# Forgetting scores negated, their mask and minimum in one VectorE instruction, the softmax division moved to the branch, and the output halves added in DRAM

## The chip, the cores and the metric

The kernel runs on one core of a Trainium2 chip. The metric is the device time of one execution in microseconds (us), smaller being better. Three executions of the kernel before took 1705.4, 1707.59 and 1708.07 us; the median is 1707.59 us.

## What is computed

One decoder block in float32 on 1024 tokens of width 1024: three gated attention branches, merged, projected and added to the residual, and then a squared-ReLU MLP. The lines that matter here:

```python
# stick-breaking: 8 heads of 64, strictly causal
log_rem = jnp.where(strict, jax.nn.log_sigmoid(-z), 0.0)
w = jnp.where(strict, jnp.exp(jax.nn.log_sigmoid(z) + after), 0.0)
# forgetting: 8 heads of 64, F = cumsum(log_sigmoid(f_logit + b_forget))
z = z + F[:, :, q0:kend, None] - F[:, :, None, :kend]
p = jax.nn.softmax(jnp.where(causal, z, NEG_INF), axis=-1)
# memory: 4 heads of 128 on 256 memory tokens, ordinary softmax
merged = gates[:, :, 0] * br_sb + gates[:, :, 1] * br_fox + gates[:, :, 2] * br_mem
x = x + jnp.einsum('bsd,de->bse', merged, w_out[l])
u = jax.nn.relu(jnp.einsum('bsd,df->bsf', h2, w_ff_up[l]))
x = x + jnp.einsum('bsf,fd->bsd', u * u, w_ff_down[l])
```

## The kernel before

Each matmul operand is split into a high and a low float32r part, and a product is the sum of three matmuls (high by high, high by low, low by high). The work has five stages: a prologue that norms and turns the tokens; the input projections; attention together with the gate projections; the three branch products and the output projection; the MLP's two products.

Up to the end of the branches the order of the instructions is not written out: the kernel runs a small planner (`Machine`) while it is built. Each piece of work is a generator that asks for a place (`Get`, a tile or a PSUM bank) or for an engine (`Op`, with an engine, an assumed cost and a function that emits the instructions). The planner emits them in the order in which its own model would start them, and the chip then runs each engine's list strictly in that order. Pieces marked `side=True`, the dense gate and branch products of L1119, are taken on TensorE only when no attention piece is ready, so they fill the gaps of attention.

The attention stage has 64 units: 4 head pairs of stick-breaking (`sb_tile`), then 4 of forgetting (`fox_tile`), each with 2 heads by 4 groups of two query blocks of 128. A unit makes two tiles of scores (128 queries by 128 to 1024 keys), in chunks of at most 512 columns, one PSUM bank each, and then, in `unit`, turns them on TensorE (L904, through the bank `tr`), splits them into `pth` (ScalarE, L909) and `ptl` (VectorE, L911), and multiplies by V (L921). V lies as high and low halves side by side, so the product has the high half's result in partitions 0 to 63 and the low half's in 64 to 127, and the two must be added.

A forgetting chunk before: two matmuls (L837, L838; the second adds F by four extra rows `fq_scr`, `fk_scr`), on the last chunk an addition of the triangle mask `above` to its last 128 columns (L843), the row maximum (L844), its negation (L845), and the exponential with the row sum accumulated (L848). A tile of two chunks then brings the chunks to one maximum with small VectorE instructions and one small exponential (L856, L858), makes 1/sum (L862 to L865), and ScalarE multiplies the tile by it (L871). A tile of one chunk has a reciprocal (L867) in place of those.

At a unit's end ScalarE copies the low half to `ob` (L939), VectorE adds the high half (L940), and SP stores the 64 by 256 result to `o_scr` (L942). `ob` has three tiles. GpSimd (POOL) issues the loads of this stage: queries and keys (L979), values (L1015), memory operands (L567, L577) and the weights of the dense work, `raw<-w_in` (L1037), which ScalarE and VectorE then split (L1029, L1030).

After attention, `bring` loads each 128 rows of a branch's `o_scr` into `raw` (L1554) and splits them; `dense_branch` runs the memory and stick-breaking branches, and `last_branch` the forgetting branch.

Of the kernel before, what the change touches and what calls it, by code (L numbers as in the profile page):

```python
# [43 lines left out]
def tile_hybrid_block(  # L44
# [40 lines left out]
    C = Pool("c", st=32, st16=8, ss=4)  # L85
# [10 lines left out]
    def mmbank():  # L96
# [6 lines left out]
    above = C.p.tile([P, P + 1], F32, tag="above", name="above")  # L103
    nc.gpsimd.memset(above, 0.0)
    nc.gpsimd.affine_select(out=above, in_=above, pattern=[[-1, P + 1]], compare_op=ALU.is_ge,
                            fill=NEG, base=0, channel_multiplier=1)
    tri, strict = above[:, :P], above[:, 1:]
# [10 lines left out]
    o_scr = [dram.tile([512, S], F32, name=f"o_scr{b}", tag=f"o_scr{b}") for b in range(3)]  # L118
    gate_scr = dram.tile([3 * D, S], F32, name="gate_scr", tag="gate_scr")
# [11 lines left out]
    def stat(n, dt=F32):  # L131
        return (C.t("st", [P, 8], dt) if n <= 8 else C.t("st16", [P, 16], dt))[:, :n]

# [203 lines left out]
    ES, OO, EL, RR, HT, PH, PL, OB, VV, BK = (Places([]) for _ in range(10))  # L337
# [127 lines left out]
    def small_loads():  # L465
# [9 lines left out]
        def scale():  # L475
            nc.vector.tensor_scalar(gq2, gq2, HD ** -0.5, None, ALU.mult)
            nc.vector.tensor_scalar(gmq, gmq, P ** -0.5, None, ALU.mult)
# [116 lines left out]

    def mem_attention(h, half, kv, q):
# [8 lines left out]
        def scores_of(t2):  # L604
# [9 lines left out]
            def maxima():  # L614
                nc.vector.tensor_reduce(mx, sc.rearrange("p (t m) -> p t m", m=MEM), AX.X, ALU.max)
                nc.vector.tensor_scalar(mx, mx, -1.0, None, ALU.mult)
# [7 lines left out]
            yield Op("DVE", dve_time(512) + SMALL, maxima)  # L624
# [161 lines left out]
    def sb_tile(pair, b, i, beta):  # L786
# [4 lines left out]
        def chunk(ci, c, m, u):  # L791
# [6 lines left out]
            def sigmoids():  # L798
                nc.scalar.activation(rho[:, c:c + u], sc[:, :u], AF.Sigmoid, scale=-HD ** -0.5)  # L799
                nc.scalar.activation(beta[:, c:c + u], sc[:, :u], AF.Sigmoid, scale=HD ** -0.5)  # L800

            yield Op("PE", mm_time(m, m), scores)
            if c + u == n:
                dg = sc[:, u - P:u]
                yield Op("DVE", 0.22, lambda: nc.vector.tensor_tensor(dg, dg, strict, ALU.add))
# [18 lines left out]
    def fox_tile(pair, b, i, e):  # L824
# [5 lines left out]
        st = stat(16)  # L830
        mx, nx, l, f, t_, m = (st[:, c0:c0 + 2] for c0 in range(0, 12, 2))

        def chunk(ci, c, cols, u):
# [6 lines left out]
            def maxima():  # L840
                if c + u == n:
                    dg = sc[:, u - P:u]
                    nc.vector.tensor_tensor(dg, dg, tri, ALU.add)  # L843
                nc.vector.tensor_reduce(mx[:, ci:ci + 1], sc[:, :u], AX.X, ALU.max)  # L844
                nc.vector.tensor_scalar(nx[:, ci:ci + 1], mx[:, ci:ci + 1], -1.0, None, ALU.mult)  # L845
            yield Op("PE", mm_time(cols, cols), scores)
            yield Op("DVE", (0.22 if c + u == n else 0.0) + dve_time(u) + SMALL, maxima)
            yield Op("ACT", act_time(u) + 0.21, lambda: nc.scalar.activation(  # L848
                e[:, c:c + u], sc[:, :u], AF.Exp, bias=nx[:, ci:ci + 1], accum_out=l[:, ci:ci + 1]), table=AF.Exp)
# [4 lines left out]
        if two:  # L854
            def most():
                nc.vector.tensor_tensor(m[:, 0:1], nx[:, 0:1], nx[:, 1:2], ALU.min)  # L856
            yield Op("DVE", SMALL, most)
            yield Op("ACT", 0.22, lambda: nc.scalar.activation(f, mx, AF.Exp, bias=m[:, 0:1]), table=AF.Exp)  # L858

        def scale():  # L860
            if two:
                nc.vector.tensor_tensor(t_, l, f, ALU.mult)  # L862
                nc.vector.tensor_tensor(m[:, 1:2], t_[:, 0:1], t_[:, 1:2], ALU.add)
                nc.vector.reciprocal(t_[:, 0:1], m[:, 1:2])
                nc.vector.tensor_scalar(f, f, t_[:, 0:1], None, ALU.mult)  # L865
            else:
# [1712 lines left out]
```

## Time and profile before

| | us |
|---|---|
| median of three runs (1705.4 to 1708.07) | 1707.59 |
| the profiled execution | 1706.93 |
| its span, first to last instruction | 1705.1 |
| around the span | 1.83 |
| attention with the gate projections, from about | 380 to 850 |

The profile shows one execution. Its groups of instructions give busy time, the mean of one instruction in ns, and the idle time of the engine just ahead of them with what ended it. Busy time by stretches of the span shows where an engine had room, the view of waits shows who waited for whom, and the chain of waits follows the work that ended last back in time. TensorE's matmuls overlap: each is shown for some 390 ns, and the next one starts after some 230 ns at 512 columns. Matmul ends are modelled, so gaps shorter than this overlap do not show as idle time.

### The profile page before, as it was taken

Reading aid. Unit: us, or ns where it says so; the run is one execution under the profiler, and the core shown is the slowest. Engines: PE = TensorE matmul, PEld = TensorE weight load, DVE = VectorE, ACT = ScalarE, POOL = GpSimd, SP = SyncE. Lnnn points to the kernel's source line nnn. Section 1 sums busy time; section 2 is a strip of 40 time slices with the busy share of each in tenths; the row PEclk is TensorE's granted clock in tenths of the full one; section 3 lists DMA queues with packets and bytes.
Section 4 is the critical chain, followed back from the end, with each engine's and each line's share of the span. In section 5 each row is a group of like instructions: output and inputs, shape, how many; then the busy total and the mean of one; then the engine's idle time right before and its main releaser. Section 6 shows DMA issues by size and latency. Waiting matters only on the chain.

```text
span 1705.1 us, 25350 instructions
## 1 busy us (share of the span) xinstructions
PE 1691.7 (99%) x9186; PEld 1442.8 (85%) x9186; DVE 1346.3 (79%) x2321; ACT 886.8 (52%) x1635; POOL 256.0 (15%) x441
## 2 busy tenths in 40 slices
PE   9999999999999999999999999999999999999998
PEld 9998899998888888888888887878888887888887
DVE  7977678868999888888656898987777776788775
ACT  6445555556676798889733446533233344332331
POOL 0000000043322233241000011021211120000000
PEclk9999999999999999999999999999999999999999
DMA  7545444576544453553375642144444484554532
GB/s 242 162 144 191 135 124 149 157 245 187 160 128 123 113 176 112 183 164 110 100 238 168 217 179 94 56 162 141 156 153 149 142 289 180 195 206 148 198 123 74
DMA packets 131406, 271.72 MB, mean 159 GB/s; under 512 B 15761, under 2 KB 43409, under 8 KB 131281
## 3 DMA queue, kind: packets, MB, share of 16 engines
q1 hardware_dynamic: 99600, 169.94, 29.2%
q0 software_dynamic: 31680, 100.17, 19.5%
q8 instruction: 72, 1.18, 0.3%
q14 instruction: 54, 0.43, 0.1%
HBM read 181.44 MB, written 88.60 MB: 158 GB/s over the span
## 4 chain that ended last, share of the span: by engine, by line
PE 83%; issue 7%; DVE 5%; DMA 2%; POOL 2%; ACT 1%; SPq 0%; POOLq 0%; DVEq 0%; ACTq 0%
PE pp L1119 21%; PE pp L2518 7%; PE pp L1405 7%; PE pp L1848 6%; PE sc L1405 5%; PE tr L904 4%; PE tr L2518 4%; PE sc L2518 4%; PE sc L1119 3%; PE sc L1848 3%; PE pv L2518 2%; PE pv L921 2%; PE pp L921 2%; PE pv L1405 2%; POOL s_scr L1865 2%
## 5 line engine op out<-in xcount | busy, mean ns | idle before, releaser
L1119 PE MATMUL pp<-hi,whi 128*128 128x512 f32 x368 | 147.6, 401 | 0.0
L1119 PE MATMUL pp<-hi,wlo 128*128 128x512 f32 x368 | 145.0, 394 | 0.0
L1119 PE MATMUL pp<-lo,whi 128*128 128x512 f32 x368 | 144.8, 393 | 0.0
L1030 DVE TENSOR_TENSOR wlo<-raw,whi 128x1024 fp32r<-128x1024 f32 (+1 forms) x82 | 100.0, 1221 | 38.9 <-ACT whi L1029 38.6
L2518 PE MATMUL pp<-h,sop 128*128 128x512 f32 x540 | 128.7, 395 | 1.4 <-DVE sop L1784 1.4
L2518 PEld LDWEIGHTS pp<-h,sop 128*128 128x128 f32 x540 | 101.1, 187 | 26.5 <-DVE sop L1784 1.8
L1848 PE MATMUL pp<-h,oh 128*128 128x512 f32 x384 | 120.9, 396 | 0.7 <-ACT cu L1934 0.6
L1029 ACT ACTIVATE whi<-raw 128x1024 fp32r<-128x1024 f32 (+1 forms) x82 | 86.8, 1059 | 52.4 <-PE pp L1405 18.7
L911 DVE TENSOR_TENSOR ptl<-tr,pth 128x512 fp32r<-128x512 f32 (+1 forms) x160 | 98.8, 627 | 11.0 <-ACT pth L909 10.6
L909 ACT ACTIVATE pth<-tr 128x512 fp32r<-128x512 f32 (+1 forms) x160 | 86.7, 558 | 28.5 <-PE tr L904 15.5
L814 DVE TENSOR_TENSOR_SCAN r<-r,sm 128x896 f32<-128x896 f32 (+4 forms) x64 | 85.5, 1345 | 3.5 <-ACT r L799 3.4
L2436 ACT ACTIVATE h<-t 128x2048 fp32r<-128x2048 f32 x16 | 30.7, 1919 | 110.4 <-DVE t L1784 97.9
L1848 PEld LDWEIGHTS pp<-h,oh 128*128 128x128 f32 x384 | 71.7, 187 | 19.2 <-ACT cu L1934 1.5
L1119 PEld LDWEIGHTS pp<-hi,wlo 128*128 128x128 f32 x368 | 69.1, 188 | 16.4
L1119 PEld LDWEIGHTS pp<-lo,whi 128*128 128x128 f32 x368 | 69.5, 189 | 10.3
L1119 PEld LDWEIGHTS pp<-hi,whi 128*128 128x128 f32 x368 | 69.4, 189 | 10.1
L1848 PE MATMUL pp<-h,ol 128*128 128x512 f32 x192 | 75.9, 396 | 0.0
L1841 ACT ACTIVATE oh<-raw 128x512 fp32r<-128x512 f32 x64 | 39.4, 625 | 61.7 <-DVE raw L1784 61.7
L2518 PE MATMUL sc<-h,sop 128*128 128x512 f32 x264 | 63.4, 395 | 0.0
L2518 PE MATMUL tr<-h,sop 128*128 128x512 f32 x264 | 63.4, 395 | 0.0
L1784 DVE TENSOR_TENSOR sop<-ur,sop 128x2048 fp32r<-128x2048 f32 x27 | 61.7, 2286 | 1.7 <-ACT sop L2447 1.7
L844 DVE TENSOR_REDUCE st<-sc 128x1 f32<-128x512 f32 (+2 forms) x96 | 53.3, 555 | 9.3 <-PE sc L838 7.1
(586 smaller groups left out, 5102.9 us busy)
## 6 DMA issues: line engine op xcount, KB each, us to landing
ur<-s_scr SPq DMA_DIRECT2D x26, 1024.0 KB
raw<-w_in POOLq DMA_DIRECT2D x42, 512.0 KB, 5.2
raw<-w_up SPq DMA_DIRECT2D x60, 256.0 KB
s_scr<-s POOLq DMA_DIRECT2D x60, 256.0 KB, 2.5
g<-w_down SPq DMA_DIRECT2D x14, 1024.0 KB
s_scr<-cu POOLq DMA_DIRECT2D x48, 256.0 KB, 2.9
gate_scr<-o SPq DMA_DIRECT2D x44, 256.0 KB
o<-gate_scr SPq DMA_DIRECT2D x32, 256.0 KB
```

The costliest lines, as they stand in the source:

```text
L814: nc.vector.tensor_tensor_scan(out=rev, data0=rev, data1=zero.to_broadcast([P, n]), initial=1.0, op0=ALU.mult, op1=ALU.add)
L904: nc.tensor.transpose(tr[:, jj * 256 + a * P:jj * 256 + (a + 1) * P], es[a][:, j * P:(j + 1) * P], ident)
L909: yield Op("ACT", act_time(512 - lo_c), lambda: nc.scalar.activation(ph[:, lo_c:], tr[:, lo_c:], AF.Copy))
L911: yield Op("DVE", dve_time(512 - lo_c), lambda: nc.vector.tensor_tensor(pl[:, lo_c:], tr[:, lo_c:], f32(ph[:, lo_c:]), ALU.subtract))
L921: nc.tensor.matmul(pv[0][:, c_:256], pair.v[:, j, b, :], p_[:, jj * 256 + c_:(jj + 1) * 256], start=(k == 0 and n_ == 0 and i == 0), stop= ...
L1029: yield Op("ACT", 0.03 + act_time(m), lambda: nc.scalar.activation(hi, raw, AF.Copy))
L1030: yield Op("DVE", dve_time(m), lambda: nc.vector.tensor_tensor(lo, raw, f32(hi), ALU.subtract))
L1119: nc.tensor.matmul(ps, a_, b_, start=(first and i == 0), stop=(last and i == n - 1))
L1405: nc.tensor.matmul(out_, a_, b_, start=(first and n == 0 and j == 0), stop=(last and n == 3 and j == len(todo) - 1), skip_group_check=True)
L1784: nc.vector.tensor_tensor(out_, a_, b_, op)
L1848: nc.tensor.matmul(ps, w[a_][:, k * P:(k + 1) * P], h[b_][k], start=(first and k == 0 and i == 0), stop=(last and k == 3 and i == 2), skip ...
L2518: nc.tensor.matmul(ps, a_[:, c, qs], b_[:, c, :], start=(kind in ("P1", "P2", "P7") and c == 0 and i == 0), stop=(kind in ("P2", "P4", "P3 ...
```

## The change

- **Scores of the forgetting heads are made negative.** The query gain gets a factor of -1, and F's rows change their signs. A row's maximum becomes a minimum, which is the bias that the exponential needs (with scale -1), so that the negation goes.
- **Mask and minimum in one instruction.** On a tile's last chunk one `tensor_tensor_reduce` adds the mask and takes the minimum. The mask is a new tile `later` of 513 columns: zeros, with the triangle in the last 129, so that a slice of it ends in the triangle for each chunk width. The stick-breaking queries are negated as well, and their mask is the same triangle. In the order below this instruction is two rows, both named ISA.
- **One minimum for both chunks.** The second chunk's exponential takes the minimum of both as its bias; the first chunk alone is brought to it afterwards, on VectorE (512 columns), which also adds the two sums.
- **1/sum leaves the tile.** The sums stay in the columns of `fn`; at the end of a pair one reciprocal of 128 by 16 is taken and stored to `l_scr` in runs of 4 bytes (`sums_kept`). `bring` loads them spread over 64 partitions each (two DMAs) and VectorE multiplies the 128 by 1024 rows before they are split.
- **Output halves added by a DMA.** ScalarE copies all 128 partitions to `ob`. SP stores the high half, and POOL then issues a DMA that adds the low half to the same place in DRAM.
- The memory heads' negation goes into the reduction's `negate`.

```diff
             def maxima():
                 if c + u == n:
-                    dg = sc[:, u - P:u]
-                    nc.vector.tensor_tensor(dg, dg, tri, ALU.add)
-                nc.vector.tensor_reduce(mx[:, ci:ci + 1], sc[:, :u], AX.X, ALU.max)
-                nc.vector.tensor_scalar(nx[:, ci:ci + 1], mx[:, ci:ci + 1], -1.0, None, ALU.mult)
+                    nc.vector.tensor_tensor_reduce(sc[:, :u], sc[:, :u], holder["later"][:, 512 - u:512], 1.0, -NEG,
+                                                   ALU.add, ALU.min, nx[:, ci:ci + 1])
+                else:
+                    nc.vector.tensor_reduce(nx[:, ci:ci + 1], sc[:, :u], AX.X, ALU.min)
...
+            if ci == 0:
+                machine.fire(first_max)
+            else:
+                yield first_max
+                bias = m
+                yield Op("DVE", SMALL, lambda: nc.vector.tensor_tensor(m, nx[:, 0:1], nx[:, 1:2], ALU.min))
             yield Op("ACT", act_time(u) + 0.21, lambda: nc.scalar.activation(
-                e[:, c:c + u], sc[:, :u], AF.Exp, bias=nx[:, ci:ci + 1], accum_out=l[:, ci:ci + 1]), table=AF.Exp)
+                e[:, c:c + u], sc[:, :u], AF.Exp, scale=-1.0, bias=bias,
+                accum_out=l[:, ci:ci + 1] if two else total), table=AF.Exp)
...
-        def scaled():
-            for ci, (c, _, u) in enumerate(ch):
-                nc.scalar.activation(e[:, c:c + u], e[:, c:c + u], AF.Copy, scale=f[:, ci:ci + 1])
-        yield Op("DVE", SMALL * (4 if two else 1), scale)
-        yield Op("ACT", act_time(*[u for _, _, u in ch]) + 0.0002 * n, scaled)
+            yield Op("ACT", 0.22, lambda: nc.scalar.activation(f, nx[:, 0:1], AF.Exp, scale=-1.0, bias=m), table=AF.Exp)
+
+            def scaled():
+                nc.vector.tensor_scalar(e[:, :512], e[:, :512], f, None, ALU.mult)
+                nc.vector.scalar_tensor_tensor(total, l[:, 0:1], f, l[:, 1:2], ALU.mult, ALU.add)
+            yield Op("DVE", dve_time(512) + SMALL, scaled)
...
-        o = ob[:HD, :]
-        yield Op("ACT", act_time(256), lambda: nc.scalar.activation(o, pv[0][HD:P, :256], AF.Copy))
-        yield Op("DVE", dve_time(256), lambda: nc.vector.tensor_tensor(o, o, pv[0][0:HD, :256], ALU.add))
+        yield Op("ACT", act_time(256), lambda: nc.scalar.activation(ob, pv[0][:, :256], AF.Copy))
         PV.put(pv[0])
-        yield Op("SP", 0.1, lambda: nc.sync.dma_start(scr[r0:r0 + HD, g * 256:(g + 1) * 256], o), 2.5)
+        dst = scr[r0:r0 + HD, g * 256:(g + 1) * 256]
+        yield Op("SP", 0.1, lambda: nc.sync.dma_start(dst, ob[:HD, :]), 3.0)
+        yield Op("POOL", 0.6, lambda: nc.gpsimd.dma_start(dst, ob[HD:, :], accum_op=ALU.add), 3.5)
         OB.put(ob)
...
+    def sums_kept(h0):
+
+        cols = fn[:, 8 * h0:8 * h0 + 16]
+        yield Op("DVE", SMALL, lambda: nc.vector.reciprocal(cols, cols))
+        yield Op("SP", 0.4, lambda: nc.sync.dma_start(
+            l_scr[h0:h0 + 2, :].rearrange("h (i p) -> p (h i)", p=P), cols, allow_slow_non_contiguous=True), 4.0)
...
+        def issue():
+            nc.sync.dma_start(raw[:, :S], src)
+            if bi == 2:
+                for i, half in enumerate((slice(0, HD), slice(HD, P))):
+                    nc.sync.dma_start(sums[half, :], l_scr[2 * k + i:2 * k + i + 1, :].partition_broadcast(HD))
+        yield from transfer(issue, P * S * (8 if bi == 2 else 4))
+        if bi == 2:
+            yield Op("DVE", dve_time(S), lambda: nc.vector.tensor_tensor(raw[:, :S], raw[:, :S], sums, ALU.mult))
+            RR.put(sums)
```

With other costs and other pieces the planner emits another order. TensorE has the same 8855 rows, ScalarE 1368 in place of 1454, VectorE 2028 in place of 2290, POOL 452 in place of 390, SP 508 in place of 500. Three places; line numbers of the order after are those of the changed file (L843, L844: the score matmuls; L905: the turns; L922: the products by V; L1122: dense and memory products; L861: the exponential).

**TensorE, the turns of the narrow tile of the last forgetting unit.** The tile is `es_4095` before, `es_4093` after, 256 keys wide. Before, the rows ahead of its turns:

```order
L921 MATMUL pp_131<-ptl_4089,v_3939 128x128
L1119 MATMUL pp_129<-hi_122,whi_161 128x512
L1119 MATMUL pp_129<-lo_123,whi_161 128x512
L1119 MATMUL pp_129<-hi_122,wlo_162 128x512
L1119 MATMUL pp_129<-hi_122,whi_161 128x512
L1119 MATMUL pp_129<-lo_123,whi_161 128x512
L1119 MATMUL pp_129<-hi_122,wlo_162 128x512
L921 MATMUL pp_131<-pth_4088,v_3939 128x256
L921 MATMUL pp_131<-ptl_4090,v_3939 128x256
L921 MATMUL pp_131<-pth_4088,v_3939 128x256
L921 MATMUL pp_131<-ptl_4090,v_3939 128x256
L904 MATMUL tr_135<-ident,es_4095 128x128
```

After, from the second matmul of its scores (`sc_129`, 256 columns) to its turns:

```order
L844 MATMUL sc_129<-whi_155,h_4104 128x256
L1122 MATMUL pp_127<-pth_4086,h_4105 128x512
L1122 MATMUL pp_127<-ptl_4088,h_4105 128x512
L1122 MATMUL pp_127<-pth_4086,h_3926 128x512
L843 MATMUL sc_128<-h_3931,h_3927 128x512
L844 MATMUL sc_128<-whi_155,h_4099 128x512
L1122 MATMUL pp_125<-hi_118,whi_159 128x512
L1122 MATMUL pp_125<-lo_119,whi_159 128x512
L1122 MATMUL pp_125<-hi_118,wlo_160 128x512
L905 MATMUL tr_130<-ident,es_4093 128x128
```

The scores moved close to the turns: eight matmuls of 512 columns lie between them after, and before the scores stand further up than the rows shown.

**VectorE, in the forgetting pairs.** `st` are small columns (maxima, sums), `ptl` the low parts of turned tiles. Before, two single chunks and the end of a tile of two:

```order
L843 TENSOR_TENSOR sc_132<-sc_132,above 128x128
L844 TENSOR_REDUCE st_6211<-sc_132 128x1
L845 TENSOR_SCALAR st_6211<-st_6211 128x1
L940 TENSOR_TENSOR ob_4092<-ob_4092,pv_136 64x256
L843 TENSOR_TENSOR sc_133<-sc_133,above 128x128
L844 TENSOR_REDUCE st_6212<-sc_133 128x1
L845 TENSOR_SCALAR st_6212<-st_6212 128x1
L862 TENSOR_TENSOR st_6190<-st_6190 128x2
L863 TENSOR_TENSOR st_6190<-st_6190 128x1
L864 RECIPROCAL st_6190<-st_6190 128x1
L865 TENSOR_SCALAR st_6190<-st_6190 128x2
```

After, single chunks and the beginning of a tile of two (L851 is the plain minimum of its first chunk, L860 the minimum of both):

```order
L848 ISA sc_128,st_6188<-sc_128,later_3943 128x256
L848 ISA st_6188 128x1
L848 ISA sc_129,st_6283<-sc_129,later_3943 128x384
L848 ISA st_6283 128x1
L912 TENSOR_TENSOR ptl_4087<-tr_130,pth_4085 128x384
L848 ISA sc_128,st_6284<-sc_128,later_3943 128x512
L848 ISA st_6284 128x1
L912 TENSOR_TENSOR ptl_4088<-tr_131,pth_4086 128x512
L851 TENSOR_REDUCE st_6355<-sc_129 128x1
L912 TENSOR_TENSOR ptl_4087<-tr_130,pth_4085 128x512
L848 ISA sc_128,st_6355<-sc_128,later_3943 128x384
```

Three rows of a chunk became two, and the additions of `ob` and the small rows of 1/sum are gone.

**POOL, behind the loads of the first memory operands.** Before:

```order
L577 DMA h_3928<-m_scr_99 128x512
L577 DMA whi_159<-m_scr_99 128x512
L979 DMA h_3933<-fxk_scr_91 64x512 x2
L979 DMA h_3930<-fxk_scr_92 64x512
L979 DMA h_3930<-fk_scr 4x512
L979 DMA h_3926<-fxk_scr_91 64x512 x2
```

After (L943 is the adding DMA, L1040 a weight load, L563 a load of memory queries):

```order
L573 DMA h_4102<-m_scr_95 128x512
L573 DMA h_3923<-m_scr_95 128x512
L943 DMA o_scr_75<-ob_4090 64x256
L943 DMA o_scr_75<-ob_4089 64x256
L943 DMA o_scr_75<-ob_4091 64x256
L1040 DMA raw_162<-w_in 128x8x128
L943 DMA o_scr_75<-ob_4090 64x256
L563 DMA h_3927<-mq_scr_89 128x512
L563 DMA h_4100<-mq_scr_90 128x512
L563 DMA wlo_156<-mq_scr_89 128x512
L563 DMA h_4099<-mq_scr_90 128x512
L943 DMA o_scr_75<-ob_4089 64x256
```

The 64 adding DMAs came between the loads, in many places directly ahead of a weight load (15 of the 22 loads `raw<-w_in`).

More of the change, by code (lines that the diff above doesn't have):

```diff
@@ L118, in tile_hybrid_block @@
     o_scr = [dram.tile([512, S], F32, name=f"o_scr{b}", tag=f"o_scr{b}") for b in range(3)]
+    l_scr = dram.tile([8, S], F32, name="l_scr", tag="l_scr")
     gate_scr = dram.tile([3 * D, S], F32, name="gate_scr", tag="gate_scr")
@@ L336, in tile_hybrid_block @@
     PP, SC, TR, PV = (banks(tag) for tag in ("pp", "sc", "tr", "pv"))
[L337 removed]
+    ES, OO, EL, RR, HT, PH, PL, OB, VV, BK, LATER = (Places([]) for _ in range(11))
     SN, RS, S1 = tiles(E, "sn", 10, 512), tiles(R, "raw", 4, 1024), R.t("s1", [P, 4, 256])
@@ L946, in unit @@
             VV.put(pair.v_)
+            if pair.kind == "fox":
+                yield from sums_kept(2 * pair.p)
             machine.fire(pair.over)
```

65 lines of the change are left out of this document (31 added, 34 removed).

## The prediction

> **What bounds the kernel now.** I read the page's busy line first, then busy time by stretches, then the waits of the stretch that the change touches, then the chain of waits at the one wait found there. The page, and the stretches from the start of attention on:
>
> ```profile
> span 1705.1 us, 25350 instructions
> PE 1691.7 (99%) x9186; PEld 1442.8 (85%) x9186; DVE 1346.3 (79%) x2321; ACT 886.8 (52%) x1635; POOL 256.0 (15%) x441
> ```
>
> ```profile
> core 0: us, PE busy (x) PEld busy (x) DVE busy (x) ACT busy (x) POOL busy (x), PEclk, DMA share, GB/s
> 380.00:580.00 200.00, 199.03 (x1174) 173.03 (x1173) 185.24 (x285) 136.86 (x300) 66.47 (x116) 1.00 0.52 147
> 580.00:850.00 270.00, 270.00 (x1617) 235.09 (x1616) 219.77 (x682) 228.05 (x577) 74.00 (x133) 1.00 0.46 140
> 850.00:940.00 90.00, 89.95 (x388) 72.66 (x387) 52.70 (x75) 31.83 (x47) 6.77 (x9) 1.00 0.61 199
> ```
>
> Two thirds of the change lies between 380 and 850 us. There VectorE is busy 405.0 of 470 us and ScalarE 364.9, which looks like the place to save. But TensorE is busy 469.0 of 470: the planner lays dense products into every gap of attention, so the stage is as long as its matmuls. At 850 to 940 us, where the sums are now multiplied in, TensorE is busy 89.95 of 90. The waits of TensorE in 380 to 860 us are one row, and the chain of waits shows how it came:
>
> ```profile
> PE sc L795 <- ACT es L800: 1.0, 1, 1.0
> ```
>
> ```profile
> 388.35 0.86 issue
> 389.21 0.39 ACT ob L939
> 389.90 0.39 ACT es L800
> 390.33 0.50 PE sc L795
> ```
>
> The first copy to `ob` (L939) could not start for 0.86 us for a reason the profile does not name; the sigmoid behind it on ScalarE was late by that, and TensorE lost 1.0 us. Two things follow. Waits of TensorE to be saved here sum to about 1.0 us, 0.06% of the run. And ScalarE passes a block on `ob` to TensorE about one to one.
>
> **The change part by part.** The work on TensorE is the same 8855 rows, so no term comes from there. For VectorE these are the rows of 362 to 860 us:
>
> ```profile
> L844 DVE TENSOR_REDUCE st<-sc 128x1 f32<-128x512 f32 (+2 forms) x96 | 53.3, 555 | 9.3 <-PE sc L838 7.1
> L843 DVE TENSOR_TENSOR sc<-sc,above 128x128 f32<-128x128 f32 x64 | 18.7, 292 | 6.8 <-PE sc L838 5.7 <-ACT pth L909 0.8
> L845 DVE TENSOR_SCALAR st<-st 128x1 f32<-128x1 f32 x96 | 14.7, 154 | 3.3
> L940 DVE TENSOR_TENSOR ob<-ob,pv 64x256 f32<-64x256 f32 x33 | 13.4, 405 | 7.6 <-ACT ob L939 7.5
> L940 DVE TENSOR_TENSOR ob<-ob,pp 64x256 f32<-64x256 f32 x31 | 12.4, 402 | 3.1 <-ACT ob L939 3.1
> L636 DVE TENSOR_SCALAR r<-r,st 128x256 f32<-128x256 f32 x32 | 9.5, 359 | 0.3
> L865 DVE TENSOR_SCALAR st<-st 128x2 f32<-128x2 f32 x32 | 7.3, 229 | 1.1
> L864 DVE RECIPROCAL st<-st 128x1 f32<-128x1 f32 x32 | 5.3, 164 | 1.1
> L863 DVE TENSOR_TENSOR st<-st 128x1 f32<-128x1 f32 x32 | 5.1, 160 | 1.1
> L867 DVE RECIPROCAL st<-st 128x1 f32<-128x1 f32 x32 | 4.9, 154 | 1.4 <-ACT es L848 1.4
> L862 DVE TENSOR_TENSOR st<-st 128x2 f32<-128x2 f32 x32 | 4.8, 151 | 2.5 <-ACT st L858 2.5
> ```
>
> Removed: 18.7 + 14.7 + 13.4 + 12.4 + 7.3 + 5.3 + 5.1 + 4.9 + 4.8 = 86.6 us. The 64 fused mask-and-minimum instructions, which no row shows, take the place of 64 of the 96 reductions; at the least they cost as those did, at the most as mask and reduction one after the other, 0.29 us more each (0 to 18.7 us). I take the lower end, since the reduction already passes over all columns. The second ISA row of each costs at least a small column's 0.154 us: 9.9 us. Scaling the first chunk of 512 columns 32 times costs at most twice L636's 0.359 us, 23.0 us, and the 32 sums 5.1 us. Added: 38 us, at most 57. So VectorE is lighter by 30 to 49 us. ScalarE loses the multiplication of the tiles:
>
> ```profile
> L871 ACT ACTIVATE e<-e,st 128x512 f32<-128x512 f32 x64 | 37.6, 639 | 2.7 <-DVE st L865 1.8 <-DVE st L856 0.6
> L871 ACT ACTIVATE es<-es,st 128x128 f32<-128x128 f32 (+3 forms) x32 | 17.7, 561 | 0.6 <-DVE st L867 0.5
> ```
>
> That is 55.3 us, while its copy to `ob` keeps its 256 columns. All this lies beside a TensorE that is busy 469 of 470 us. **It is worth between 0 and 1.0 us**, and I take 0: the one wait hangs on the first `ob` copy, which stays.
>
> Added waits. At a unit's end there are now two DMAs in series, the second in POOL's queue behind a wait for the first. SP's landings are not shown; the nearest rows are POOL's stores to DRAM of 256 KB (`s_scr`, L1865):
>
> ```profile
> L1865 POOL DMA_DIRECT2D s_scr<-s x60: 542/542/552, 1119.2 to 1389.9; - x60
> DMA to landing us min/median/max: 2.3/2.7/7.6
> ```
>
> ```profile
> L942 SPq DMA_DIRECT2D o_scr<-ob x64: 445/446/559, 390.1 to 845.4; - x64
> ```
>
> ```profile
> 864.20 5.57 PE sc L1119 x24
> ...
> 936.61 2.78 PE pp L1119 x12
> ```
>
> Issue 0.45, landing 2.7, issue 0.54, landing 2.7 and the copy's 0.4 make 6.8 us until an `ob` tile is free; with the longest landings 16.6. By the matmuls' spacing (5.57 us / 24 = 0.232 us) the unit ends that share an `ob` tile lie at least 8.5 us apart in the new order, and 3 of 61 under 11 us. So at the median landing no copy waits, and at the longest a few wait up to 8 us, which the chain above says would reach TensorE. I take one block of the kind seen, **+1.0 us**, since the median row is nearer than the maximum; the bounds are 0 and, were all three to meet the longest landings, 8.1 + 6.2 + 5.7 = 20 us. POOL itself has room: 64 x 0.54 = 35 us more on 140 of 470.
>
> The Trainium skill, "DMA: Bandwidth & Descriptors", section "Anatomy of one DMA — SWDGE (gpsimd) path", gives a DMA about 2.0 us fixed plus bytes / 436e3. An estimate by it for these 64 KB is 2.15 us, and for the 256 KB stores 2.6, where the trace has a median of 2.7; by it alone an `ob` tile comes free in about 5.7 us, no copy waits and this term is 0. The 7.6 us in the same row is not in the rule, and the row decides. The page's "Two DMAs through the same engine are not ordered" speaks against the change: the adding DMA cannot just be queued behind the store, its issuer must wait.
>
> Closer chains. With fewer steps the planner puts a tile's turns nearer to its scores. Counted in matmuls at 0.232 us, the shortest of the 64 forgetting tiles had 7.6 us before; now the last one has 8 x 0.232 = 1.9 us, one more 2.3 us, and the rest 3.9 us or more. What must fit for 256 keys:
>
> ```profile
> L844 DVE TENSOR_REDUCE st<-sc 128x1 f32<-128x256 f32 x16 | 6.8, 424 | 0.5
> L848 ACT ACTIVATE es<-sc,st 128x256 f32<-128x256 f32 x8 | 3.8, 475 | 1.1 <-DVE st L845 0.9
> ```
>
> 0.42 + 0.15 + 0.48 = 1.05 us, 1.34 with the mask's 0.29 on top, plus whatever stands ahead on the two engines. It fits by 0.5 to 0.8 us; I take **+0.5 us** for the two tightest together, with bounds of 0 and 64 x 0.1 = 6 us.
>
> Cost nothing: the four multiplications of 128 by 1024 by the sums (about 1.2 us each by L636's rate, 5 us) and 2 MB more of loads, since VectorE is busy 52.7 of 90 us there and the rows are wanted only when the other branches' products, whose last piece in the chain starts at 936.61 us, are through. If that cover were gone, one such row would cost its 1.2 us. The four stores of sums in 4-byte runs have no row; the last is 28 transfers ahead of its first reader on SP, so even 10 us would not show. The sign changes only replace instructions by others of the same width.
>
> **Sum.** The profiled execution took 1706.93 us, its span of 1705.1 and 1.83 around it. 1706.93 + 0 + 1.0 + 0.5 = 1708.4; the median of the runs lies 0.66 us higher, so 1709.1, given as 1709.0 us: no change that a measurement shows. About 0.2%, 3.4 us, is what a measurement of this kernel can tell from no change, so that "same" is 1704.2 to 1711.0.
>
> **The rivals.** *POOL's queue holds up the loads (slower).* 15 of the 22 weight loads now stand right behind an adding DMA, which waits for its store's landing, up to 7.6 us. ScalarE takes the weights in its own order, and it already waited for them before:
>
> ```profile
> L1029 ACT ACTIVATE whi<-raw 128x1024 fp32r<-128x1024 f32 x23 | 24.4, 1063 | 4.0 <-DMA raw<-w_in 3.8 <-DMA raw<-w_b 0.2
> ```
>
> Against it: none of those 3.8 us reached TensorE. For it: the block on `ob` did, one to one. It decides from the point at which a store's landing exceeds its usual 2.7 us by about a microsecond in more than a few units. With ten blocks of the 0.9 us seen: 1707.6 + 9 = 1716.6 us. Chance 0.28.
>
> *The fused instruction costs more than its parts,* or the closer chains miss by a little everywhere: 64 tiles by 0.1 us is 1714 us. For it: the shortest distance fell from 7.6 to 1.9 us. Against it: all but two are still 3.9 us and more. Chance 0.14.
>
> *Hidden waits go (faster).* Matmul ends are modelled, and a wait shorter than the overlap of two matmuls (0.39 us shown, 0.23 us apart) does not show as idle. If 30 such of 0.15 us went, 1707.6 - 4.5 = 1703 us. Against it: the planner fills with dense work whatever the length of a chain. Chance 0.06.
>
> *It doesn't do what it says:* at the upper end of the fused instruction's price, VectorE saves 30 us, not 49. The time is the forecast's, since VectorE is not the bound; 0.08, inside "same".
>
> **How the numbers follow.** The forecast has 0.44, and with the last rival "same" has 0.52; slower 0.28 + 0.14 = 0.42; faster 0.06. The range runs from 1705.0 us (the one wait gone, no term added, and an execution as low as the lowest before) to 1720.0 (beyond the first rival, about half of the 20 us bound on blocked copies and all of the 6 us on close chains); the rest of those bounds is in the 0.2 left outside.
>
> **What would show it.** Right: TensorE busy about 469 of 470 us in the attention stage again, VectorE there lighter by 30 to 49 us and ScalarE by about 55, with no gain in time. The `ob` term shows as idle time of ScalarE before `ob` released by a DMA; the queue rival as POOL's waits at the adding DMA and ScalarE's at `whi<-raw` with TensorE waiting for `pth` or `es` behind them; the second rival as TensorE's turns waiting for ScalarE's `es` or `e`. The prediction is wrong if TensorE's waits in the stage sum to over 4 us, or if the stage gets shorter by more than its 1 us of idle time.

## The result and the profile after

| | us |
|---|---|
| after, median of four runs (1727.54 to 1732.07) | 1728.08 |
| before, median of four runs beside them | 1707.83 |
| after / before, 95% interval | 1.0125 (1.0105 to 1.0144) |
| the profiled execution after, its span | 1727.54, 1725.4 |

The change made the kernel slower by 1.25%, outside the range of the prediction. The page after, its busy line:

```profile
span 1725.4 us, 25186 instructions
PE 1697.9 (98%) x9186; PEld 1448.9 (84%) x9186; DVE 1296.8 (75%) x2057; ACT 832.3 (48%) x1539; POOL 314.7 (18%) x505
```

VectorE has 49.5 us less to do and ScalarE 54.5, as the change says. The stretches say where the time went all the same (after the span's share come the granted clock, the DMA share and GB/s):

```profile
core 0: us, PE busy (x) PEld busy (x) DVE busy (x) ACT busy (x) POOL busy (x), PEclk, DMA share, GB/s
380.00:580.00 200.00, 200.00 (x1194) 174.47 (x1193) 183.22 (x270) 137.95 (x311) 89.00 (x144) 1.00 0.60 155
580.00:850.00 270.00, 258.30 (x1536) 224.53 (x1535) 169.62 (x431) 171.84 (x469) 107.74 (x170) 0.97 0.63 138
```

The stick-breaking half (380 to 580 us) is whole, although 28 of the 64 adding DMAs stand in it. In the forgetting half TensorE now has 11.7 idle us and a clock of 0.97, where it had none and 1.00; the DMA share rose from 0.46 to 0.63, while the bytes moved per second stayed (140 before, 138 now). So the DMA engines are busy with something that moves few bytes; the runs below split the rise into the stores of the sums and the addition. TensorE's waits from 362 to 900 us, where before had one of 1.0 us:

```profile
PE sc L843 <- ACT e L861: 5.8, 2, 5.3
PE tr L905 <- ACT es L861: 3.1, 1, 3.1
PE sc L843 <- ACT r L623: 2.8, 1, 2.8
PE sc L1122 <- ACT whi L1032: 2.1, 1, 2.1
PE sc L797 <- ACT e L802: 1.1, 1, 1.1
PE sc L1122 <- DVE wlo L1033: 0.5, 1, 0.5
```

Four long stalls, then, near 620, 698, 750 and 856 us (the wait of 1.1 us lies ahead of 380 us). All name ScalarE; the chain of waits (start, length, what) shows what ScalarE waited for. The first stall:

```profile
619.93 3.41 issue
623.34 0.38 ACT ob L939
...
623.94 0.49 DVE e L872
...
624.99 0.20 ACT e L861
...
626.03 3.75 PE pp L1122 x9
```

A copy to `ob` could not start, and the exponential behind it came late. The nine matmuls after it take 0.417 us each instead of 0.232: TensorE came back at half speed. The third and the fourth stall:

```profile
730.01 10.82 DMA o_scr<-ob
...
744.52 6.28 DMA raw<-w_in
...
839.73 16.82 DMA raw<-w_in
...
858.94 12.15 PE sc L1122 x46
```

Here single transfers take 10.82 us (64 KB) and 16.82 us (512 KB; the median of this load is 5.3). They begin 6.5 us behind the second, and together with the fourth, of the stores of the sums (SP issues these at 652.7, 723.5, 787.4 and 839.9 us). The chain of the second stall leads back to the time of the first store by a longer road: a store to `o_scr` of 6.45 us at 659.0, POOL's queue behind it, and a weight load of 9.93 us at 688.3. TensorE's row there, turns waiting for `es`, is the sign that the prediction gave for closer chains; the chain shows that the load was what came late.

### The profile page after: what moved, and what is told of

Same layout as the page of the kernel before. It is cut to its first block, busy times and chain, and to the rows that moved or that the text cites. A ratio compares the mean times of both kernels' runs of the same rounds, so it can differ in the third digit from the quotient of the medians.

```text
span 1725.4 us, 25186 instructions
## 1 busy us (share of the span) xinstructions
PE 1697.9 (98%) x9186; PEld 1448.9 (84%) x9186; DVE 1296.8 (75%) x2057; ACT 832.3 (48%) x1539; POOL 314.7 (18%) x505
## 4 chain that ended last, share of the span: by engine, by line
PE 72%; issue 14%; DMA 6%; POOL 4%; DVE 2%; ACT 1%; SPq 0%; POOLq 0%; ACTq 0%; DVEq 0%
PE pp L1122 17%; PE pp L2542 7%; PE pp L1408 7%; PE sc L1408 5%; PE sc L2542 4%; PE tr L2542 4%; PE sc L1122 3%; PE tr L905 3%; DMA raw<-w_in 3%; POOL s_scr L1889 3%; PE pv L2542 2%; PE pv L1408 2%; PE pp L922 2%; PE pv L922 2%; PE pp L1872 1%
## 5 line engine op out<-in xcount | busy, mean ns | idle before, releaser
L1122 PE MATMUL pp<-hi,whi 128*128 128x512 f32 x352 | 143.0, 406 | 0.0
L1122 PE MATMUL pp<-hi,wlo 128*128 128x512 f32 x352 | 140.3, 399 | 0.0
L1122 PE MATMUL pp<-lo,whi 128*128 128x512 f32 x352 | 140.0, 398 | 0.0
L943 POOL DMA_DIRECT2D o_scr<-ob x64 | 54.2, 890 | 226.9 <-DMA o_scr<-ob 70.3
L817 DVE TENSOR_TENSOR_SCAN r<-r,sm 128x896 f32<-128x896 f32 (+5 forms) x64 | 85.4, 1349 | 9.1 <-ACT r L801 9.1
L1122 PEld LDWEIGHTS pp<-hi,wlo 128*128 128x128 f32 x352 | 67.0, 190 | 15.8
L1122 PEld LDWEIGHTS pp<-lo,whi 128*128 128x128 f32 x352 | 67.4, 191 | 9.7
L1122 PEld LDWEIGHTS pp<-hi,whi 128*128 128x128 f32 x352 | 67.5, 192 | 9.5
L1325 POOL DMA_DIRECT2D raw<-w_in x20 | 15.2, 758 | 282.8 <-DVE wlo L1033 282.8
```

Of the source, the lines that this page charges most:

```text
L817: nc.vector.tensor_tensor_scan(out=rev, data0=rev, data1=zero.to_broadcast([P, n]), initial=1.0, op0=ALU.mult, op1=ALU.add)
L943: yield Op("POOL", 0.6, lambda: nc.gpsimd.dma_start(dst, ob[HD:, :], accum_op=ALU.add), 3.5)
L1122: nc.tensor.matmul(ps, a_, b_, start=(first and i == 0), stop=(last and i == n - 1))
```

## The experiments

Two theories stood at the start. **Theory 1:** the stores of the sums in 4-byte runs hold up every other transfer for some 10 us each. **Theory 2:** the adding DMA in POOL's queue, with three `ob` tiles, holds up `ob` and the loads. A third cause, the fused instruction or the closer chains, was kept in view. Times are medians; ratios are to before, run on the same chip.

| run | us | ratio, 95% interval |
|---|---|---|
| after | 1728.08 | 1.0125 (1.0105 to 1.0144) |
| e1_runs64: sums in 64-byte runs | 1718.19 | 1.0067 (1.0052 to 1.0082) |
| e2_twice: 4-byte stores twice | 1759.65 | 1.0315 (1.0295 to 1.0335) |
| e3_vector_add: halves added on VectorE | 1714.78 | 1.0054 (1.0039 to 1.0069) |
| e5_rows_vector_add: both undone | 1707.10 | 1.0005 (0.9992 to 1.0018) |
| e6_before_stores: before, with 4-byte stores | 1717.86 | 1.0058 (1.0043 to 1.0073) |
| e7_before_dma_add: before, with adding DMA | 1710.76 | 1.0029 (1.0019 to 1.0038) |
| e8_no_add: e1, POOL's DMA does not add | 1717.14 | 1.0053 (1.0038 to 1.0068) |
| e9_no_wait: e1, POOL's DMA need not wait for the store | 1710.88 | 1.0021 (1.0006 to 1.0037) |
| e10_sp_low: e1, nothing of ob on POOL | 1708.99 | 1.0006 (0.9996 to 1.0016) |
| e11_five_ob: e1, five ob tiles | 1713.26 | 1.0043 (1.0026 to 1.0059) |
| e12_later_add: e1, adding DMA planned later | 1707.06 | 1.0007 (0.9994 to 1.0020) |
| e13_rows_later_add: all computed, both causes gone | 1709.11 | 1.0004 (0.9993 to 1.0015) |

### The stores of the sums: e1, e2, e6

**e1_runs64**, the same instructions on every engine, another pattern in DRAM:

```diff
-            l_scr[h0:h0 + 2, :].rearrange("h (i p) -> p (h i)", p=P), cols, allow_slow_non_contiguous=True), 4.0)
+            l_scr[h0:h0 + 2, :].rearrange("h (a c) -> (h a) c", c=16), cols), 4.0)
```

> The changed kernel with one edit: the four stores of the sums write l_scr in runs of 64 bytes, 128 of them, in place of 2048 runs of 4 bytes (the sums then lie in another order in DRAM, so that the multiplication by them takes sums of other queries). Every engine's list stays the same, row by row. Theory 1, the 4-byte stores hold up all other transfers for about 10 us each and so cause three of the four long stalls of TensorE (those near 700, 752 and 858 us of the span): 1714 to 1718 us, and no half-speed clock at those places; the stall near 623 us, which lies before the first of these stores, stays. Theory 2, the adding DMA in POOL's queue and the three ob tiles cause the stalls: within 0.2% of the changed kernel, 1725 to 1731.

1718.19 us, 9.9 below after: 0.2 above theory 1's range, and far from theory 2's. Busy time and DMA in the 10 us behind the first store, after and then e1:

```profile
653.00:663.00 10.00, 10.00 (x63) 8.82 (x63) 6.57 (x17) 7.08 (x19) 0.00 (x0) 1.00 0.90 57
```

```profile
653.00:663.00 10.00, 10.00 (x64) 8.81 (x63) 6.54 (x16) 7.04 (x18) 1.51 (x3) 1.00 0.23 76
```

The same stretch with the same list of instructions: a share of 0.90 for 57 GB/s after, 0.23 for 76 in e1. TensorE's waits in e1, 580 to 960 us:

```profile
PE sc L843 <- ACT e L861: 6.3, 2, 5.0
PE sc L147 <- DVE o L1677: 2.9, 1, 2.9
```

The stalls near 698, 750 and 856 us are gone (a third row, 0.3 us, is not shown); the one near 620 stayed, which lies ahead of the first store. The wait of 2.9 us at the branch is new and is taken up below.

**e2_twice**, each store issued twice:

```diff
-        yield Op("SP", 0.4, lambda: nc.sync.dma_start(
-            l_scr[...], cols, allow_slow_non_contiguous=True), 4.0)
+        yield Op("SP", 0.4, lambda: [nc.sync.dma_start(
+            l_scr[...], cols, allow_slow_non_contiguous=True) for _ in "12"], 4.0)
```

> The changed kernel with each of the four stores of the sums issued twice, one directly behind the other; the order on every engine is otherwise the same. Theory 1 (4-byte stores hold up the other transfers): each stop of the transfers lasts 20 us in place of 10, and TensorE loses at least as much again as it lost behind the stores, 1738 to 1760 us. Theory 2 (adding DMA and ob tiles): 1725 to 1731 us.

1759.65 us, 31.6 above after and at the upper end of what was expected. The chain of waits has the store itself, which no earlier trace showed:

```profile
652.67 10.30 DMA l_scr<-fn
...
664.42 11.51 DMA o_scr<-ob
```

A store of 8 KB takes **10.30 us** until it has landed, and the 64 KB store behind the second one 11.51. The run overstates a plain doubling: the second store writes the same place, waits on SP for the first, and so holds SP's queue as well.

**e6_before_stores**, the kernel before with four such stores that nothing reads:

```diff
             VV.put(pair.v_)
+            if pair.kind == "fox":
+                yield Op("SP", 0.4, lambda: nc.sync.dma_start(
+                    l_scr[2 * pair.p:2 * pair.p + 2, :].rearrange("h (i p) -> p (h i)", p=P), ident[:, :16],
+                    allow_slow_non_contiguous=True), 4.0)
             machine.fire(pair.over)
```

> The kernel before with four stores of 2048 runs of 4 bytes added, one at the end of each forgetting pair (16 columns of the identity to a spare place in DRAM; nothing reads them), and nothing else of the change. If a store of this kind holds up all transfers by itself: 1711 to 1719 us, with the weights (raw from w_in) landing late behind it. If the stop only matters because POOL then waits at an adding DMA with the loads behind it: 1705 to 1709 us.

1717.86 us, 10.1 above before: these stores alone cost what e1 saved, with no adding DMA near. Its stores issue at 662.5, 725.2, 795.7 and 850.3 us, and the chain shows what stood behind the last two:

```profile
798.82 11.39 DMA raw<-o_scr
...
856.16 9.45 DMA gate_scr<-o
866.10 4.29 DMA o<-gate_scr
```

Theory 1 is shown, by taking the runs of 4 bytes away, by doubling them, and by adding them alone. The Trainium skill, "DMA: Bandwidth & Descriptors", section "Rules for kernel authors", says that a non-contiguous last dimension becomes one descriptor per element and should be rearranged. The traces agree: packets under 512 bytes rise from 15761 in before to 24017 in e6, by 8256, and four stores of 2048 elements are 8192. They add what this does to the neighbours: 11.39 us for the load of 512 KB above, 10.82 for a store of 64 KB after.

### The adding DMA: e3, e5, e7

**e3_vector_add** keeps the 4-byte stores; **e5_rows_vector_add** has the same edit, and turns the sums on TensorE and stores 16 rows of 512 bytes:

```diff
-        yield Op("ACT", act_time(256), lambda: nc.scalar.activation(ob, pv[0][:, :256], AF.Copy))
...
-        yield Op("POOL", 0.6, lambda: nc.gpsimd.dma_start(dst, ob[HD:, :], accum_op=ALU.add), 3.5)
+        yield Op("ACT", act_time(256), lambda: nc.scalar.activation(o, pv[0][HD:P, :256], AF.Copy))
+        yield Op("DVE", dve_time(256), lambda: nc.vector.tensor_tensor(o, o, pv[0][0:HD, :256], ALU.add))
...
+        yield Op("PE", 0.1, lambda: nc.tensor.transpose(tr[:16, :P], cols, ident))
+        yield Op("DVE", SMALL, lambda: nc.vector.tensor_copy(rows, tr[:16, :P]))
+        yield Op("SP", 0.1, lambda: nc.sync.dma_start(
+            l_scr[h0:h0 + 2, :].rearrange("h (i p) -> (h i) p", p=P), rows), 2.5)
```

> The changed kernel with the output halves added as before (ScalarE copies one half, VectorE adds the other, one store on SP; no adding DMA), and the 4-byte stores of the sums kept. The planner's order changes with it. Theory 1 (4-byte stores): only the stall near 623 us and what it costs in clock go, 7 to 9 us; 1717 to 1722 us. Theory 2 (adding DMA and ob tiles): nearly all of the loss goes, 1706 to 1711 us. If neither holds but the fused instruction or the closer chains cost the time: 1725 to 1731.

> The changed kernel with both undone: halves added on VectorE as before, and the sums turned on TensorE (one 128 by 16 transpose per pair) and stored as 16 rows of 512 bytes. What stays of the change: negated scores, the fused mask and minimum, one minimum for both chunks, the division at the branch. Theories 1 and 2 both expect the time before, 1705 to 1711 us. If the fused instruction or the closer chains cost time by themselves: 1714 us or more.

e3 took 1714.78 us, lower than theory 1 alone allowed and higher than theory 2: both causes are real. e5 took 1707.10, no different from before, and TensorE has no wait in 380 to 940 us. So the fused minimum, the closer chains and the division at the branch together cost nothing that can be measured, and the third cause falls. Against e5, the stores cost 7.7 us (e3) and the adding DMA at most 11.1 (e1, where some 4.5 lie at the branch, see below); together after has 21.0.

The medians near before hide one more place. Where the MLP begins, TensorE waits 3.3 us for `h` in e5, 3.7 in e12 and 3.3 in e13, and then has some 3.4 us at half clock; before waits 1.6 us there and keeps its clock. Up to this wait these executions are 0.4 to 2.0 us ahead of before. So the savings may be worth up to 2 us, which are lost again there; executions of one kernel differ by more than this, so that single ones can't show it.

**e7_before_dma_add**, the adding DMA alone on the kernel before (the edit of the diff in the section on the change):

> The kernel before with the output halves added by POOL's DMA, and nothing else of the change (VectorE's additions of the halves go). If the place of the adding DMA in POOL's queue costs by itself: 1714 to 1721 us, with a wait of ScalarE ahead of an ob copy or of TensorE behind late loads. If it costs only together with the other order that the shorter chains of the change bring: 1706 to 1711 us.

1710.76 us, at the upper end of its second range: 4.8 above before, and the interval of its ratio leaves out 1. So the DMA costs by itself too, less than in the order of the change. The trace has the same place: POOL stands, a burst of loads follows, ScalarE's copy to `ob` is late, TensorE waits 1.6 us, and the clock falls behind it.

```profile
601.60 0.83 POOL L942 DMA_DIRECT2D o_scr<-ob  x1 [8.38 <-ACT e L871]
```

```profile
620.40:623.80 3.40, 3.40 (x10) 2.54 (x10) 2.06 (x10) 3.39 (x9) 0.03 (x1) 0.51 0.72 217
```

### What in the adding DMA costs: e8 to e12

All five stand on e1, so that the 4-byte runs are out. **e8_no_add** only drops the addition; every list is the same:

```diff
-nc.gpsimd.dma_start(dst, ob[HD:, :], accum_op=ALU.add)
+nc.gpsimd.dma_start(dst, ob[HD:, :])
```

> The kernel with stores of 64-byte runs, and POOL's DMA of the low half no longer adds but overwrites the same place (the output loses the high halves' products). Every engine's list is the same, POOL still waits for the high half's store. If the adding itself is what costs (its issue of 0.84 us, its slower packets): 1706 to 1712 us. If it is the place of this DMA in POOL's queue, behind the loads, and the wait ahead of it: 1715 to 1720 us, with TensorE's stall near 623 us still there.

1717.14 us, with the stall near 620 us still there (5.6 us). The addition itself costs POOL 0.31 us of issue, the rows of e1 and of e8, and it is not what hurts:

```profile
L943 POOL DMA_DIRECT2D o_scr<-ob x64: 802/838/1211, 400.5 to 830.6; - x64
```

```profile
L943 POOL DMA_DIRECT2D o_scr<-ob x64: 527/532/563, 398.8 to 830.2; - x64
```

**e9_no_wait** puts the low half elsewhere, so that POOL need not wait for SP's store; **e10_sp_low** lets SP issue that store:

```diff
-yield Op("POOL", 0.6, lambda: nc.gpsimd.dma_start(dst, ob[HD:, :], accum_op=ALU.add), 3.5)
+low = o_low[r0:r0 + HD, g * 256:(g + 1) * 256]
+yield Op("POOL", 0.6, lambda: nc.gpsimd.dma_start(low, ob[HD:, :]), 3.5)      # e9
+yield Op("SP", 0.1, lambda: nc.sync.dma_start(low, ob[HD:, :]), 3.0)          # e10
```

> The kernel with stores of 64-byte runs, and POOL's DMA puts the low half to a place of its own without adding (the output loses the low halves' products), so that it need not wait for the high half's store. Every engine's list is the same but for numbers of buffers. If the wait for the store in POOL's queue causes the remaining loss: 1706 to 1711 us. If it is the burst of loads that stands ahead of this DMA in POOL's queue while ob waits for it: 1713 to 1719 us, with the stall near 623 us still there.

> As the run before this one, but the low half's store to its own place is issued by SP right behind the high half's, so that nothing of ob stands in POOL's queue (the output loses the low halves' products). The planner's order changes with it. If POOL's queue causes the remaining loss: 1705 to 1710 us and no stall near 623 us. If three ob tiles of 128 partitions are too few anyhow, or the planner's closer chains matter: 1713 to 1719 us.

e9: 1710.88 us, at the edge of its first range, and scattered (1705.71 to 1720.28). The profiled execution is the lowest of the ten, so it shows this run at its best. POOL stands in it as long as in e1 at the same DMA (9.85 us; 9.57 in e1), now for the copy to `ob` alone, and the same loads leave behind it. The DMA's row, and the rows of the copy's line from 595 to 632 us:

```profile
597.76 0.53 POOL L943 DMA_DIRECT2D o_low<-ob  x1 [9.85 <-ACT ob L939]
```

```profile
L939 ACTq EVENT_SEMAPHORE  x6: 38/38/4637, 595.8 to 629.8; - x6
```

The DMA leaves at 597.8 us, where e1 has 600.6; ScalarE's longest wait for `ob` is 4.6 us in place of 7.8, and TensorE's wait near 620 us is 1.9 in place of 5.0. So in that execution the wait for the store is about 3 of the 5 us of this stall, and the DMA's place in POOL's queue is the rest. e10: 1708.99, within 0.2% of before, so nothing measurable is left with POOL's queue free of `ob`. Its order differs and its interval meets that of e9, so that it doesn't price the place in the queue by itself. POOL's instructions in order of time, after (start, length, idle time ahead of it and what ended it):

```profile
589.62 1.21 POOL L1040 DMA_DIRECT2D raw<-w_in  x1
600.82 0.84 POOL L943 DMA_DIRECT2D o_scr<-ob  x1 [9.99 <-ACT es L861]
601.38 1.41 POOL L982 DMA_DIRECT2D whi<-fxk_scr  x2
...
611.25 0.91 POOL L1018 DMA_DIRECT2D v<-v_fx  x1
...
614.13 1.06 POOL L573 DMA_DIRECT2D h<-m_scr  x2 [0.91 <-DMA whi<-fxq_scr]
615.19 0.94 POOL L943 DMA_DIRECT2D o_scr<-ob  x1
```

POOL stands for 9.99 us at an adding DMA: until its unit's copy to `ob`, which begins at 597.4 us, and then for the store of the high half. The loads of a whole forgetting pair are stuck behind it. Then they leave in one burst from 601.4 to 615.2 us, 1 MB of V among them, and the next unit's adding DMA, whose store had issued by 606, comes behind the burst. What that did to `ob`, by the rows of the copy's line from 595 to 630 us, and by those of the adding DMA's line from 615.0 to 615.9 us:

```profile
L939 ACTq EVENT_SEMAPHORE  x5: 38/38/8103, 596.0 to 615.2; - x5
```

```profile
L943 POOL DMA_DIRECT2D o_scr<-ob x1: 935/935/935, 615.2 to 615.2; - x1
...
DMA to landing us min/median/max: 8.1/8.1/8.1
```

ScalarE waits 8.1 us from 615.2 us on for an `ob` tile, until 623.3: the adding DMA issued at 615.19 took the 8.1 us to land behind that burst.

**e11_five_ob** and **e12_later_add**, two ways out:

```diff
-        opened("A2", (PH, "pth", 2, 512, F32R), (PL, "ptl", 2, 512, F32R), (OB, "ob", 3, 256, F32),
-               (ES, "es", 4, 512, F32), (OO, "o", 3, 512, F32), (HT, "h", 7, 512, F32R))
+        opened("A2", (PH, "pth", 2, 512, F32R), (PL, "ptl", 2, 512, F32R), (OB, "ob", 5, 256, F32),
+               (ES, "es", 4, 512, F32), (OO, "o", 3, 512, F32), (HT, "h", 6, 512, F32R))    # e11
...
-        yield Op("SP", 0.1, lambda: nc.sync.dma_start(dst, ob[:HD, :]), 3.0)
+        yield Op("SP", 0.1, lambda: nc.sync.dma_start(dst, ob[:HD, :]), 7.0)                 # e12
```

> The kernel with stores of 64-byte runs and five ob tiles in place of three (one of the 19 operand tiles h given up for them, so that the planner's order changes a little). If POOL's wait reaches TensorE by an ob tile that is not free: 1706 to 1712 us, and no wait of ScalarE ahead of an ob copy. If it reaches TensorE by loads that come late behind the adding DMA: 1714 to 1720 us.

> The kernel with stores of 64-byte runs, and the planner told that the high half's store lands after 7.0 us in place of 3.0, so that it puts the adding DMAs later in POOL's list, behind more of the loads. If POOL standing at the adding DMA while loads queue up behind it is what costs: 1707 to 1713 us. If the adding DMA standing behind loads while ob waits is what costs: 1716 to 1724 us.

e11: 1713.26 us, between its ranges. ScalarE no longer waits ahead of an `ob` copy (its longest such wait is 0.038 us), yet TensorE still waits 3.2 us for `e`; the run is 4.9 us below e1, so `ob` was the road for a part, and this run does not settle the rest, since a tile `h` went as well. e12: 1707.06 us, in its first range and no different from before; ScalarE waits nowhere for `ob` (0.038 us at the longest). POOL in e12 at the same place:

```profile
588.51 1.08 POOL L943 DMA_DIRECT2D o_scr<-ob  x1
589.07 1.64 POOL L982 DMA_DIRECT2D whi<-fxk_scr  x2
...
600.38 0.52 POOL L982 DMA_DIRECT2D h<-fq_scr  x1
603.03 0.84 POOL L943 DMA_DIRECT2D o_scr<-ob  x1 [2.14 <-DMA o_scr<-ob]
```

The adding DMA of that place now stands behind the loads of queries and keys; these leave from 589 us on, and POOL waits 2.14 us. Its waits of this kind on landings still sum to 55 us over the stage in e12 (70 after): the sum says little; what is gone at this place is the burst of loads behind a wait. The planner moved rows on the other engines as well, so e12 shows a way out rather than the cause alone; the cause rests on e1, e8 and e9, whose rows are the same on every engine but for the place that POOL's DMA writes to.

### Both causes away: e13

**e13_rows_later_add** is after with the sums' rows of e5 and the 7.0 of e12:

> The changed kernel, all of its computation kept, with both causes taken away in the way that costs least: the sums turned on TensorE and stored as 16 rows of 512 bytes, and the planner told that the high half's store lands after 7.0 us in place of 3.0 (the adding DMAs stay). If the two causes found are all: 1705 to 1709 us, the time before, TensorE without a wait of over 1 us between 580 and 850 us. If the lighter VectorE and ScalarE are worth something after all once nothing holds up the transfers: under 1703 us. If the order of the run with stores of 64-byte runs was luck: 1712 us or more.

1709.11 us, 0.1 above its first range and 1.0004 (0.9993 to 1.0015) of before. Its stretch:

```profile
580.00:850.00 270.00, 269.60 (x1614) 234.88 (x1613) 172.49 (x437) 177.06 (x476) 107.46 (x170) 1.00 0.55 150
```

TensorE is busy 269.60 of 270 us again, with VectorE lighter by 47 us than before and ScalarE by 51 in this stretch alone, and the time is that of before. No third cause is left that can be measured, and no version measurably beats the kernel before.

## Why the prediction was wrong

The forecast of 1709.0 lies next to the 1709.11 of e13, but that is luck: e13 is another kernel, and 1.5 us of the forecast are terms that it does not show. The change as made is 19 us slower.

- **Bound by TensorE, savings worth nothing: right as far as the runs can tell.** e5 and e13 show it, but for the up to 2 us that the wait at the MLP's beginning may hide.
- **The fused instruction: right, at its lower end.** The groups after:

```profile
L848 DVE CUSTOM_DVE_ANT_0 sc<-sc,later 128x512 f32<-128x512 f32 x16 | 11.1, 696 | 3.3 <-PE sc L844 3.2
L851 DVE TENSOR_REDUCE st<-sc 128x1 f32<-128x512 f32 x32 | 22.0, 687 | 8.2 <-PE sc L844 7.7
L872 DVE TENSOR_SCALAR e<-e,st 128x512 f32<-128x512 f32 x32 | 15.5, 484 | 14.0 <-ACT st L869 14.0
```

At 512 columns it takes 696 ns, the plain reduction 687; its second row has a mean of 141 ns where 154 was taken, and scaling 512 columns takes 484 where at most 720 was.
- **The four stores of sums "cost nothing": the step that failed.** The prediction weighed "even 10 us" against the reader of the sums, 28 transfers later. The length that it named in passing was right (10.30 us), and the reader did not care. But the transfers of everybody else, put at nothing, were late during it: weights, `o_scr`, gates. That costs 9.9 us by e1, 10.1 by e6 and 7.7 by e3 against e5.
- **The `ob` term of +1.0 us: mis-sized.** The mechanism was right, a copy to `ob` that ScalarE waits for and that reaches TensorE. It measured 5.3 us in one place, out of a wait of ScalarE of 8.1: not one to one, since TensorE had other work for the first 4.7 us and the steps behind the copy added 1.9. The reasoning with landing times alone (6.8 us from copy to free tile) left out that the adding DMA also stands in line on POOL, some 9 us from 606 to 615, and that behind the burst it lands after 8.1 us. The bound of 20 us would have covered it.
- **The first rival, POOL's queue, at 1716.6 us: happened too,** as at most 11.1 us (e1 against e5), in which the `ob` stall above is counted again. Its direction was half right: the loads came late behind the adding DMA, and then the next adding DMA came late behind the loads. Its test, a landing about a microsecond over 2.7, was not the point that decides: POOL stood 9.99 us, most of it for a unit that had not ended, and about 3 us for the store (e9).
- **Closer chains, +0.5 us, with bounds to 6: nothing.** e5 and e13 have the shorter chains of the change and no wait of TensorE over 0.4 us in the forgetting units.
- **Multiplications at the branch: hidden in after and e5, not in e1 and e8.** In e1 TensorE waited 2.9 us there, on this chain:

```profile
930.55 7.28 DMA r<-l_scr
937.96 1.24 DVE raw L1577
...
943.61 5.27 DMA o<-gate_scr
...
950.31 0.51 PE sc L147
```

The multiplication takes the 1.2 us forecast; the load of the sums, spread over partitions, with 7.28 us was not thought of, and a load of gates of 5.27 us follows in the chain. With the half clock behind it (1.6 us) this is some 4.5 us of e1. It is not a matter of order: after, e1, e8 and e9 run the same rows, and after and e9 have no wait there, nor have e12 and e13. What decides it stays open.

The prediction named the sign of its own failure, TensorE's waits in the stage above 4 us: they sum to 14.3 from 380 to 860 us, and to 15.4 with the wait ahead of it. Less the 1.0 us of before, and with four stretches of half clock (below: three of 1.6 us and one of 1.8), the 15.4 make 21 us; the span grew by 20.3.

## What to carry to other kernels

A transfer's cost is not only the wait of its reader: count its runs, and ask which transfers share the DMA engines with it during that time. A DMA that must wait is placed in an in-order queue as any other instruction is: look for what stands behind it, and give the planner a landing time with room for a busy queue, not the best one; here 7.0 in place of 3.0 us, a value that was tried and not read from a trace, took the ratio from 1.0067 to 1.0007. And when a change removes work from engines that are not the bound, look at its side effects on transfers first: here they moved the time, and the savings did not.

## What the runs showed of the hardware

- A store of 2048 runs of 4 bytes takes 10.30 us for 8 KB, and transfers beside it are longer by some 6 to 12 us: 64 KB stores took 10.82 and 11.51 us where the adding DMA of that size has a median of 2.7, 512 KB loads 11.39 and 16.82 where 5.3 is the median of the weight loads. In 64-byte runs the same bytes disturb nothing that can be measured (e12).
- An adding DMA of 64 KB issues in 0.84 us on POOL, a plain one in 0.53. From 580 to 850 us the DMA engines are busy for a share of 0.55 with the addition (e1) and 0.49 without (e8), at 144 GB/s in both; with the stores of 4-byte runs as well it is 0.63 (after). The times of e8 and e1 agree within their intervals.
- A stall costs more than its length. After, three stretches (first the wait near 698 us itself, then two behind waits):

```profile
698.00:701.00 3.00, 1.23 (x8) 1.14 (x9) 1.23 (x1) 2.79 (x9) 0.00 (x0) 1.00 0.01 3
701.10:704.50 3.40, 3.40 (x13) 2.72 (x12) 2.26 (x6) 2.50 (x7) 1.74 (x4) 0.52 0.34 119
858.10:861.50 3.40, 2.92 (x8) 2.08 (x7) 2.01 (x2) 1.45 (x3) 0.00 (x0) 0.52 0.75 228
```

Each of the three waits of 2.6 to 3.1 us (2.1 and 0.5 taken together at 856 us) is followed by 3.4 us at a granted clock of 0.52, near 752 us as in the rows shown, which costs 3.4 x 0.48 = 1.6 us more; the first stall has 3.8 us of it in the row of nine matmuls. The length of a wait alone does not decide whether the clock falls: behind the wait of 1.6 us in e7 it did (0.51), behind those of 1.9 us in e9 and 2.3 us at the branch in e8 it stayed at 1.00. The Trainium skill, "TensorE: Matmul & The Clock Gate", section "What's actually happening", has the clock fall after an idle window of about 3.4 us and come back after a busy one of about 3.4 us. The stretch of 3.4 us at half clock agrees; that waits of 1.6 to 3.1 us were enough is less than it says, and the measurement decides.
